# A decoder block with a 16,384-expert mixer: 16 tokens gathered on eight partitions each in place of 32 on four

## The chip, the cores and the metric

The kernel runs on one core of one Trainium2 chip. The metric is the device time of one launch in microseconds (us). Engine names are those of the profile: PE is the matrix engine (PEld its weight loads), DVE the vector engine, ACT the scalar engine, POOL the general engine GpSimd, SP the engine that only issues transfers. Engines run their own instruction queues in order and meet at semaphores.

## The reference, cut to what matters

512 tokens of width 2048 go through a mixing block (gated projections and windowed attention) and then through a PEER layer: each token has 8 heads of 16 chosen experts out of 16,384, and each expert is one row of `expert_down` and one of `expert_up` (2048 values each).

```
q = (h @ w_query).reshape(T, 8, 2, 128)             # scores against 2 x 128 sub keys
...                                                 # top 16 of each half, top 16 of their sums
experts = e1 * 128 + e2;  gates = softmax(top_v)
u  = expert_down[experts]                           # (token, 8, 16, 2048)
a  = gelu(einsum('cd,chkd->chk', h, u))
vt = expert_up[experts]
out = einsum('chk,chkd->cd', gates * a, vt)
```

All is float32. A residual sum and a last normalization follow.

## The kernel before

Tokens are treated in one of two ways.

**Dense.** For `TD` = 352 tokens (`TD = TL - EX`, three blocks of 128 less the last `EX` = 32 tokens) the kernel multiplies with all experts. The 16,384 experts are 128 blocks of 128. `down(b)` multiplies block b of `expert_down` with the `TD` token columns and takes the gelu. `up(c)` multiplies eight blocks (a chunk) of `expert_up` with the gelus, each first multiplied by a gate table g that is zero where a token did not choose the expert. In `up` there are four quarters q; each has four weight pieces, and adds its result into `accT`. Every float32 product is three matmuls of split operands (`mm3`, lines 166 to 168: high by high, high by low, low by high). So each `down` and each eighth of a chunk is 48 matmuls with a moving operand of 128 partitions by `TD` columns.

**Gathered.** The first block of 128 tokens, and the `EX` tokens left over, are done row by row instead. One *unit* is one half row (1024 values) on 128 partitions: GpSimd issues an indirect transfer (line 706, 512 KB), and DVE either multiplies and sums it against the token (`expert_down`, line 720) or adds it, weighted, into `half_row` (`expert_up`, line 732). For the first block a partition is a token, with 128 experts, so 4 x 128 = 512 units. For the `EX` = 32 tokens, each is spread over P // EX = 4 partitions with 32 experts each: 4 x 32 = 128 units, and `finish_last` adds the four partial sums at the end.

**The weight stream** (class `Stream`). Weights come in pieces of 128 x 1024 (512 KB) through SP into `wraw` (4 buffers). ACT casts a piece to its high part `whi` (line 143), and DVE or GpSimd subtracts to get the low part `wlo` (line 145); four buffers each. `W.get(ahead)` hands out a piece and first issues the splits of up to `ahead` more pieces (2 by default). 24 matmuls use one piece.

**The pacer** (class `Pace`). The order of the work beside the matmuls is laid out when the program is built. Each `mm3` credits `vector` with 0.98 of its planned matmul time (3 x columns x 0.4505 ns), and everything on DVE is charged in planned ns. While `vector` is positive the pacer issues the table work (`paced`, when due), one unit per `gap`, or other leftovers. A split goes to DVE when `vector` is positive (charge 1250), else to GpSimd (charge 500). From the last gate table on, `spread` sets `gap` so that the units left are spread evenly over the matmuls left.

**The stages.** First the mixing block, the projections and the choice of experts. Then `down` of blocks 0 to 87 (`NPRE` = 88); beside the first 83 of them (`OPEN`) the gate tables are made for the dense tokens, four tokens at a time (a quad: four DVE products at line 860, eight small matmuls at line 873) and stored in `g_dram`, `NTG` groups of 32 tokens. The gelus of these 88 blocks go out to `a_dram`. Then chunks 0 to 9 of `up`, one after the other, for which gelus and tables are loaded back and multiplied (`make_ga`: the product at line 994, the cast at 998, the low part at 999). From block 88 on eight `down` and one `up` alternate, and `make_ga` is called in `down`. In the last chunk, `finish_first` (its second part is `rest_of_first`) finishes the first block, `finish_last` the `EX` tokens, and `rows_out` turns `accT` back into rows, adds and normalizes.

## Time and profile before

| | us |
|---|---|
| median of 3 runs (lowest, highest) | 3057.38 (3054.41, 3064.22) |
| the profiled execution | 3053.1 |
| its span, first to last instruction | 3051.4 |
| PE busy | 2867.4 (94%) |
| DVE busy | 2260.2 (74%) |
| POOL busy | 1474.2 (48%) |
| ACT busy | 1152.7 (38%) |
| mean granted clock of PE | 0.976 |

The profiled execution is 4.3 us below the median. Busy times are unions of an engine's instructions; those of PE are partly modelled, since matmuls overlap in the pipeline, so the pace of the matmuls is better read from the distance between their starts. A group's row gives its busy time, the mean duration of one, and the idle time just before its instructions with what ended it.

### The profile page before, as it was taken

How to read it: one execution, taken by the hardware profiler on the slowest of the kernel's cores; microseconds unless marked ns; L12 is line 12 of the kernel's file. 1: busy time of each engine (PE TensorE's matmuls, PEld its weight loads, DVE VectorE, ACT ScalarE, POOL GpSimd, SP SyncE). 2: the span in 40 equal slices, each digit the busy share in tenths (PEclk: the TensorE clock that was granted, in tenths of full speed). 3: DMA queues.
4: the chain of work that ended last, by engine and by line, in shares of the span. 5: the costliest groups of instructions: out<-in, count | busy, mean ns of one | idle time of the engine just before them, and what ended most of it. 6: DMA issues, size and time to landing. Idle time of an engine off the chain costs nothing. (4 is left out here: it accounts for less than half of the span.)

```text
span 3051.4 us, 44502 instructions
## 1 busy us (share of the span) xinstructions
PE 2867.4 (94%) x16925; PEld 2727.1 (89%) x16925; DVE 2260.2 (74%) x3359; ACT 1152.7 (38%) x1932; POOL 1474.2 (48%) x998
## 2 busy tenths in 40 slices
PE   7999999999999899999989999999999999999976
PEld 6888878799999899999988999998999999999975
DVE  3125642469947999999957888887788889778865
ACT  3244432222333456767824222322232323323223
POOL 2132100123578667777645666666665444344432
PEclk9999999999999999999999999999999999999987
DMA  5221242422379678978798999999989999899983
GB/s 191 86 83 56 76 162 90 146 90 87 122 260 343 215 264 293 317 261 316 264 333 323 357 347 342 337 334 329 353 330 347 334 334 360 315 332 335 347 306 104
DMA packets 265190, 779.91 MB, mean 256 GB/s; under 512 B 25488, under 2 KB 94416, under 8 KB 259408
## 3 DMA queue, kind: packets, MB, share of 16 engines
q1 hardware_dynamic: 151952, 382.75, 36.7%
q0 software_dynamic: 92160, 335.59, 29.0%
q10 hardware_dynamic: 20864, 58.74, 5.0%
q8 instruction: 133, 2.18, 0.3%
q14 instruction: 81, 0.66, 0.1%
HBM read 726.20 MB, written 50.77 MB: 255 GB/s over the span
## 5 line engine op out<-in xcount | busy, mean ns | idle before, releaser
L145 POOL TENSOR_TENSOR wlo<-wraw,whi 128x1024 fp32r<-128x1024 f32 x284 | 701.0, 2477 | 849.1 <-ACT whi L143 813.3
L143 ACT CAST whi<-wraw 128x1024 fp32r<-128x1024 f32 x628 | 641.2, 1048 | 679.3 <-PE up L167 326.8
L168 PE MATMUL up<-gah,wlo 128*128 128x352 f32 x2048 | 673.9, 329 | 47.2 <-POOL wlo L145 44.0
L166 PE MATMUL up<-gah,whi 128*128 128x352 f32 x2048 | 675.2, 330 | 19.9 <-DVE accT L1092 19.2
L145 DVE TENSOR_TENSOR wlo<-wraw,whi 128x1024 fp32r<-128x1024 f32 x344 | 462.1, 1350 | 305.5 <-ACT whi L143 303.8
L166 PE MATMUL dn<-h2d,whi 128*128 128x352 f32 x2048 | 667.3, 326 | 15.2 <-ACT whi L143 15.2
L168 PE MATMUL dn<-h2d,wlo 128*128 128x352 f32 x2048 | 669.7, 327 | 5.8 <-POOL wlo L145 3.6
L167 PE MATMUL up<-gal,whi 128*128 128x352 f32 x2048 | 668.9, 327 | 0.0
L167 PE MATMUL dn<-h2d,whi 128*128 128x352 f32 x2048 | 667.0, 326 | 0.0
L168 PEld LDWEIGHTS up<-gah,wlo 128*128 128x128 f32 x2048 | 394.0, 192 | 56.9 <-POOL wlo L145 53.2
L166 PEld LDWEIGHTS up<-gah,whi 128*128 128x128 f32 x2048 | 394.4, 193 | 27.5 <-DVE accT L1092 18.0
L166 PEld LDWEIGHTS dn<-h2d,whi 128*128 128x128 f32 x2048 | 390.8, 191 | 16.1 <-ACT whi L143 16.1
L168 PEld LDWEIGHTS dn<-h2d,wlo 128*128 128x128 f32 x2048 | 389.5, 190 | 10.3 <-POOL wlo L145 6.9
L167 PEld LDWEIGHTS up<-gal,whi 128*128 128x128 f32 x2048 | 394.7, 193 | 0.0
L167 PEld LDWEIGHTS dn<-h2d,whi 128*128 128x128 f32 x2048 | 389.7, 190 | 0.0
L720 DVE SCALAR_TENSOR_TENSOR row<-row,half_row 128x1024 f32<-128x1024 f32 x236 | 282.6, 1211 | 70.0 <-DMA row<-in_down_rows,idx 55.7
L860 DVE SCALAR_TENSOR_TENSOR p<-iota,eT,gT 128x256 fp32r<-128x256 f32 x352 | 317.0, 959 | 1.9 <-PE tr L873 1.9
L706 POOL DMA_INDIRECT row<-in_down_rows,idx x236 | 249.3, 1056 | 140.5 <-DVE row L720 88.7
L706 POOL DMA_INDIRECT more<-in_up_rows,idx x160 | 184.4, 1152 | 162.0 <-DVE half_row L732 136.3
L706 POOL DMA_INDIRECT row<-in_up_rows,idx x160 | 182.9, 1143 | 145.3 <-DVE half_row L732 115.7
L732 DVE SCALAR_TENSOR_TENSOR half_row<-more,wgt,half_row 128x1024 f32<-128x1024 f32 x160 | 205.1, 1282 | 1.5 <-DMA more<-in_up_rows,idx 0.3
L732 DVE SCALAR_TENSOR_TENSOR half_row<-row,wgt,half_row 128x1024 f32<-128x1024 f32 x156 | 200.0, 1282 | 1.7 <-DMA row<-in_up_rows,idx 0.3
(201 smaller groups left out, 3755.7 us busy)
## 6 DMA issues: line engine op xcount, KB each, us to landing
wraw<-in_down SPq DMA_DIRECT2D x256, 512.0 KB, 5.6
wraw<-in_up SPq DMA_DIRECT2D x256, 512.0 KB, 7.0
wraw<-in_win SPq DMA_DIRECT2D x52, 512.0 KB, 3.8
g_dram<-stage ACTq DMA_DIRECT2D x22, 1024.0 KB, 8.2
g<-g_dram SPq DMA_DIRECT2D x32, 704.0 KB, 9.3
wraw<-in_wout SPq DMA_DIRECT2D x32, 512.0 KB, 3.7
wraw<-in_wq SPq DMA_DIRECT2D x32, 512.0 KB, 3.7
aa<-a_dram SPq DMA_DIRECT2D x88, 176.0 KB, 9.1
```

Of the source, the lines that this page charges most:

```text
L143: self.nc.scalar.copy(hi, src)
L145: eng.tensor_sub(lo, src, hi.bitcast(F32))
L166: nc.tensor.matmul(ps, wh, xh, start=start, stop=False)
L167: nc.tensor.matmul(ps, wh, xl, start=False, stop=False)
L168: nc.tensor.matmul(ps, wl, xh, start=False, stop=stop)
L706: nc.gpsimd.indirect_dma_start(out=t, out_offset=None, in_=src, in_offset=bass.IndirectOffsetOnAxis(ap=idx[i][:, j, h:h + 1], axis=0))
L720: nc.vector.scalar_tensor_tensor(t, t, 1.0, half_row, op0=OP.mult, op1=OP.mult, accum_out=dots[i][:, j, h:h + 1])
L732: nc.vector.scalar_tensor_tensor(half_row, t, wgt[i][:, j:j + 1], half_row, op0=OP.mult, op1=OP.add)
L860: nc.vector.scalar_tensor_tensor(p2[:, j], iota[:, None, :].to_broadcast([P, 2, P]), t[:, 1, k:k + 1], hl[:, k, :, None].to_broadcast([P, ...
```

## The change

`EX` becomes 16 and `TD` so 368. The 16 tokens are spread over eight partitions each with 16 experts each, which makes 4 x 16 = 64 units in place of 128 (576 in all in place of 640). 368 is eleven and a half groups of 32, so there are 12 groups in `g_dram`; the last is half filled, its rest set to zero by GpSimd, and `make_ga` multiplies the last 16 columns on GpSimd and the other 352 on DVE. `NPRE` goes to 80 and `OPEN` to 75: chunks 0 to 8 run in a row, and from block 80 on `down` and `up` alternate. Buffers for gathered rows in the later stages go from 4 + 4 to 4 + 3. The pacer's first gap is 2800 ns, a split goes to DVE already when `vector` is over -400, and in each quarter of `up` the pacer issues nothing beside the last two column groups (`held`). `down` and the first half of each quarter of `up` ask for splits three pieces ahead. In the last chunk `rest_of_first` moves from the second quarter to the third; `finish_last` loads the partial sums as two transfers of 128 partitions and adds the eight parts with a matmul against a matrix of ones in place of eight DVE additions.

```diff
-EX = 32
+EX = 16
 TD = TL - EX
-NPRE = 88
+NPRE = 80
 OPEN = NPRE - 5
-NTG = TD // TG
+NTG = -(-TD // TG)
+FULL = TD // TG
-MORE_ROWS = 4
+MORE_ROWS = 3
...
-        self.gap = 2600.0
+        self.gap = 2800.0
...
-        if self.vector > 0.0 or self.pool < 0.0:
+        if self.vector > -400.0 or self.pool < 0.0:
             self.vector -= 1250.0
...
+                            used = TD - b * P - 4 * n
+                            if used < TG:
+                                nc.gpsimd.memset(stage[h][:, :, used:], 0.0)
...
-                    if n % 8 == 7:
+                    if n % 8 == 7 or 4 * (n + 1) == TD - b * P:
...
-        t3 = t.rearrange("p (g t) -> p g t", g=NTG)
         g = g4[b // 4][:, :, (b % 4) * TG:(b % 4 + 1) * TG]
-        nc.vector.tensor_tensor(t3, t3, g, op=OP.mult)
+        if FULL < NTG:
+            end = t[:, FULL * TG:]
+            nc.gpsimd.tensor_tensor(end, end, g[:, FULL, :TD - FULL * TG], op=OP.mult)
+        t3 = t[:, :FULL * TG].rearrange("p (g t) -> p g t", g=FULL)
+        nc.vector.tensor_tensor(t3, t3, g[:, :FULL], op=OP.mult)
...
-            hi, lo = W.get()
+            hi, lo = W.get(3)
...
-                w = W.get()
+                w = W.get(3)
...
-            if last and q == 1:
+            if last and q == 2:
                 rest_of_first()
-            if last and q == 2:
                 pace.drain()
                 rest_of_last = finish_last()
...
             for m in range(4):
+                pace.held = m > 1
...
+            pace.held = False
...
-            for s in range(P // EX):
-                ...
-                eng.dma_start(t[:n], y_dram[1][s * n:(s + 1) * n, cols])
-                parts.append((t, cols))
+            t = pg.tile([P, D // 2], F32, name="row", bufs=4)
+            nc.sync.dma_start(t, y_dram[1][:, h * D // 2:(h + 1) * D // 2])
+            parts.append(t)
+        ones = late["fin"].tile([P, EX], F32, name="ones")
+        nc.vector.tensor_reduce(ones, ident.rearrange("p (s m) -> p m s", m=EX), axis=AX.X, op=OP.add)
...
-            for t, cols in parts:
-                nc.vector.tensor_add(x[:n, cols], x[:n, cols], t[:n])
             for q in range(4):
+                cols = slice(q * 512, (q + 1) * 512)
+                ps = ps2.tile([P, 512], F32, name="dn", bufs=2)
+                nc.tensor.matmul(ps[:n], ones, parts[q // 2][:, q % 2 * 512:(q % 2 + 1) * 512],
+                                 start=True, stop=True)
+                nc.vector.tensor_add(x[:n, cols], ps[:n], x[:n, cols])
```

## Rows read from the trace of the kernel before

**Rows 1.** The page: span, busy time of three engines, and the span in 40 slices (granted clock of PE, busy share of the transfer engines, in tenths).

```profile
span 3051.4 us, 44502 instructions
...
PE 2867.4 (94%) x16925; PEld 2727.1 (89%) x16925; DVE 2260.2 (74%) x3359; ACT 1152.7 (38%) x1932; POOL 1474.2 (48%) x998
...
PEclk9999999999999999999999999999999999999987
DMA  5221242422379678978798999999989999899983
```

**Rows 2.** Busy time by engine in stretches of the span, the boundaries being the first matmuls of a stage: stretch, length, busy us of each engine (and instructions), granted clock, busy share of the transfer engines, GB/s.

```profile
0.00:784.00 784.00, 751.46 (x3877) 637.83 (x3877) 378.40 (x908) 264.50 (x460) 151.93 (x96) 1.00 0.30 106
784.00:1541.00 757.00, 734.11 (x4702) 728.82 (x4702) 674.87 (x992) 430.50 (x886) 559.05 (x318) 0.98 0.78 271
1541.00:1593.40 52.40, 41.59 (x239) 39.76 (x237) 29.83 (x45) 13.04 (x19) 17.63 (x16) 0.90 0.99 372
1593.40:2287.60 694.20, 643.96 (x3840) 630.85 (x3841) 564.79 (x717) 208.74 (x261) 429.94 (x301) 0.97 0.91 339
2287.60:2929.10 641.50, 622.43 (x3842) 618.20 (x3841) 542.71 (x619) 200.00 (x245) 288.41 (x242) 0.99 0.93 337
2929.10:3029.80 100.70, 72.40 (x425) 70.72 (x423) 63.19 (x71) 30.33 (x53) 25.03 (x22) 0.85 0.51 184
3029.80:3051.40 21.60, 1.41 (x9) 0.92 (x9) 6.41 (x12) 5.61 (x9) 2.21 (x6) 0.58 0.37 134
```

**Rows 3.** Matmul groups over the span (line, tiles, shapes, count; busy us, mean ns of one, overlapping; idle before), and in the timeline the first and last of ten matmuls in a row with 384 columns (start, duration).

```profile
L166 PE MATMUL up<-gah,whi 128*128 128x352 f32 x2048 | 675.2, 330 | 19.9 <-DVE accT L1092 19.2 <-ACT whi L143 0.4 <-ACT accT L1090 0.3
L166 PE MATMUL dn<-h2d,whi 128*128 128x352 f32 x2048 | 667.3, 326 | 15.2 <-ACT whi L143 15.2
L1145 PE MATMUL dn<-ident,accT 128*128 128x128 f32 x32 | 4.4, 274 | 0.3 <-DVE accT L1092 0.3
...
700.16 0.34 PE L166 MATMUL acc<-h2d,whi 128*128 128x384 f32 x1
...
701.72 0.34 PE L166 MATMUL acc<-h2d,whi 128*128 128x384 f32 x1
```

**Rows 4.** The timeline of ACT: the gelus that end a `down`, first and last of eight in a row in the late stage, and two neighbours beside the tables.

```profile
2371.72 0.47 ACT L1037 ACTIVATE aa<-dn 128x352 f32<-128x352 f32 x1 [6.79 <-PE dn L168]
...
2425.48 0.46 ACT L1037 ACTIVATE aa<-dn 128x352 f32<-128x352 f32 x1 [2.26 <-PE dn L168]
1443.29 0.47 ACT L1033 ACTIVATE asp<-dn 128x352 f32<-128x352 f32 x1 [0.45 <-PE dn L168]
1452.77 0.46 ACT L1033 ACTIVATE asp<-dn 128x352 f32<-128x352 f32 x1 [0.45 <-PE dn L168]
```

**Rows 5.** Who waited for whom in the stretch of the ten chunks, 1593 to 2287 us: total, times, longest.

```profile
DVE gal L999 <- ACT gah L998: 49.7, 81, 2.5
PE up L168 <- POOL wlo L145: 39.4, 22, 3.8
PE up L166 <- DVE accT L1092: 10.1, 11, 2.6
```

**Rows 6.** Groups of DVE and of POOL in the same stretch.

```profile
L145 DVE TENSOR_TENSOR wlo<-wraw,whi 128x1024 fp32r<-128x1024 f32 x89 | 147.2, 1659 | 37.1 <-ACT whi L143 36.7
L732 DVE SCALAR_TENSOR_TENSOR half_row<-row,wgt,half_row 128x1024 f32<-128x1024 f32 x69 | 88.4, 1282 | 0.9 <-DMA row<-in_up_rows,idx 0.3
L1092 DVE TENSOR_TENSOR accT<-up,accT 128x352 f32<-128x352 f32 x142 | 72.7, 518 | 39.1 <-PE up L168 38.8
L994 DVE TENSOR_TENSOR aa<-aa,g 128x352 f32<-128x352 f32 x81 | 46.6, 575 | 0.0
L999 DVE TENSOR_TENSOR gal<-aa,gah 128x352 fp32r<-128x352 f32 x81 | 42.5, 525 | 49.7 <-ACT gah L998 49.7
L145 POOL TENSOR_TENSOR wlo<-wraw,whi 128x1024 fp32r<-128x1024 f32 x72 | 173.0, 2414 | 167.2 <-ACT whi L143 139.9 <-issue 18.1 <-PE up L167 8.5
```

**Rows 7.** Groups of DVE and POOL in the alternating stage, 2287 to 2929 us.

```profile
L145 DVE TENSOR_TENSOR wlo<-wraw,whi 128x1024 fp32r<-128x1024 f32 x156 | 189.9, 1220 | 38.1 <-ACT whi L143 37.3 <-PE dn L168 0.9
L706 POOL DMA_INDIRECT more<-in_up_rows,idx x84 | 98.8, 1176 | 121.8 <-DVE half_row L732 113.9 <-DVE more L720 4.2 <-DVE wlo L145 2.2
```

**Rows 8.** Groups of DVE and of POOL beside the first `down` blocks, 784 to 1593 us.

```profile
L860 DVE SCALAR_TENSOR_TENSOR p<-iota,eT,gT 128x256 fp32r<-128x256 f32 x352 | 317.0, 959 | 1.9 <-PE tr L873 1.9
L720 DVE SCALAR_TENSOR_TENSOR row<-row,half_row 128x1024 f32<-128x1024 f32 x160 | 191.9, 1211 | 54.7 <-DMA row<-in_down_rows,idx 54.5
L145 POOL TENSOR_TENSOR wlo<-wraw,whi 128x1024 fp32r<-128x1024 f32 x162 | 403.7, 2497 | 158.0 <-ACT whi L143 156.5
```

**Rows 9.** The last chunk: the timeline of DVE where `rest_of_first` and `finish_last` run, and what PE waited for from 2929 us on.

```profile
2963.82 2.29 DVE L1160 TENSOR_TENSOR yf<-yf,xf 128x2048 f32<-128x2048 f32 x1 [7.72 <-DMA xf<-x_dram]
...
2972.84 0.75 DVE L1128 TENSOR_SCALAR yf<-yf,rstd 128x1024 f32<-128x1024 f32 x1 [3.51 <-POOL rstd L1126]
...
3004.48 4.95 DVE L1184 TENSOR_TENSOR xf<-xf,more 32x1024 f32<-32x1024 f32 x4
3009.36 4.95 DVE L1184 TENSOR_TENSOR xf<-xf,row 32x1024 f32<-32x1024 f32 x4
...
PE dn L1145 <- DVE xr L1148: 25.6, 4, 16.1
```

**Rows 10.** The small transfers that spread the last tokens' indices, on SP: duration least, median, most (ns), first and last start.

```profile
L931 SPq DMA_DIRECT2D idx<-e_dram x4: 302/416/422, 1374.8 to 1378.0; - x4
```

More of the change, by code (lines that the diff above doesn't have):

```diff
@@ L1171, in finish_last @@
         for h in range(2):
-            cols = slice(h * D // 2, (h + 1) * D // 2)
-            for s in range(P // EX):
-                if h:
-                    t = pg.tile([P, D // 2], F32, name="row", bufs=4)
-                else:
-                    t = late["p"].tile([P, D // 2], F32, name="more", bufs=MORE_ROWS)
-                eng = nc.sync if s % 2 else nc.scalar
-                eng.dma_start(t[:n], y_dram[1][s * n:(s + 1) * n, cols])
-                parts.append((t, cols))
+            t = pg.tile([P, D // 2], F32, name="row", bufs=4)
[3 more added lines that the diff above has]
+        nc.vector.tensor_reduce(ones, ident.rearrange("p (s m) -> p m s", m=EX), axis=AX.X, op=OP.add)
         def rest():
-            for t, cols in parts:
-                nc.vector.tensor_add(x[:n, cols], x[:n, cols], t[:n])
             for q in range(4):
+                cols = slice(q * 512, (q + 1) * 512)
[3 more added lines that the diff above has]
+                nc.vector.tensor_add(x[:n, cols], ps[:n], x[:n, cols])
                 square(NB, n, x, q, nc.vector)
```

## Prediction

> **What bounds the kernel now.** I read the page first. PE is busy 94% of the span at a clock of nearly 2.4 GHz throughout [rows 1]; so PE is the engine to account for, but its busy time is modelled, and I asked the starts of matmuls instead.
>
> In the late stage eight gelus that end a `down` lie 53.76 us apart from first to last [rows 4]: 7.68 us for 48 matmuls, 160.0 ns for one of 352 columns. That is a pace without any gap. Ten matmuls of 384 columns lie 1.56 us apart from first to last, 173.3 ns each [rows 3]. So 32 columns cost 13.3 ns (one column per cycle of 2.4 GHz), on top of a fixed 13.3 ns, and 160 ns is no floor under which 352 columns happen to lie.
>
> With that I split the span [rows 2] into what PE needs without gaps and what is lost.
>
> - 0 to 784 us, before the experts: 784.0, hardly touched.
> - 784 to 1593.4, 88 `down` and the tables: 809.4. The `down` need 88 x 7.68 = 675.8. Beside the tables two neighbours end 9.48 us apart [rows 4], 1.80 more than 7.68 for two quads, so 0.90 per quad and 78.8 for 88 quads (I take 0.895). Lost: 54.8.
> - 1593.4 to 2287.6, ten chunks: 694.2, needed 10 x 61.44 = 614.4. Lost: 79.8, or 8.0 a chunk.
> - 2287.6 to 2929.1, 40 `down` and five chunks: 641.5, needed 614.4. Lost: 27.1.
> - 2929.1 to 3029.8, the last chunk and the rows out: 100.7, needed 61.4. Lost: 39.3.
> - 21.6 of tail.
>
> About 200 us are thus lost after 784 us. Where are they? In the ten chunks PE waits 39.4 us in 22 waits for low parts that GpSimd splits, and 10.1 for DVE's additions into `accT` [rows 5]; the granted clock there is 0.97 [rows 2], so another 3% of 694, 21 us, go to half clock after such waits. In the alternating stage, with nearly every split on DVE, 156 of them [rows 7], little is lost. In the last chunk 25.6 us are waits of the row transposes for DVE [rows 9], which sits 7.7 us on a late transfer and then does 9.9 us of additions.
>
> **The change, part by part.** *Columns.* 352 to 368 adds 16 / 2.4 = 6.67 ns: 166.7 a matmul, 8.00 us a `down`, 64.0 a chunk. For 2 x 6144 matmuls (2048 of each of the three kinds, twice [rows 3]) that is 81.9 us, wherever PE has no gap to put it in. This is the cost that everything else has to earn back.
>
> *Tables.* 92 quads in place of 88: 3.6 us on PE. On DVE 16 more products of 0.96 us [rows 8], 15 us, in a stage where DVE is busy 675 of 757 us [rows 2].
>
> *Eight `down` later.* 80 `down` before the chunks take 640.0, and the quads 82.3. DVE has less time there: the pacer's plan for the table stage goes from 83 x 7.61 = 632 to 75 x 7.96 = 597 us. Quads come first, so units give way. About 150 units are done before the spread now (160 in the first four buffers up to the chunks [rows 8]). Plan time falls 34, the quads take 8 more, splits on GpSimd 8 less, and the new threshold sends perhaps a quarter of 150 splits to DVE, at 0.75 more each some 20 to 28: together 54 to 62 us, or 43 to 49 units of 1.26. I take 107 units done. The losses of the stage should stay: 52 of 54.8, since one piece more of splits at hand shortens the waits a little. The 16 small index transfers of the last tokens in place of eight cost SP 8 x 0.42 = 3.4 us [rows 10], which four loaded pieces cover. Sum: 774.3.
>
> *Units.* 576 - 107 = 469 are left at the spread, before about 490. The gap is (8304 x 352 x 0.4505 ns - 45 us) / 490 = 2.60 us now and (8688 x 368 x 0.4505 ns - 45 us) / 469 = 2.98 us after. That is where the 16 tokens fewer arrive: 21.4 units a chunk in place of 23.
>
> *Splits.* In a chunk of the row of ten, the plan credits 59.7 us now and charges 8 x 1.06 for `make_ga`, 16 x 0.52 for `accT`, 23 x 1.26 units and 16 x 1.25 splits: 65.8. The 6.1 too many divided by 0.75 is eight splits sent to GpSimd; the trace has 72 in ten chunks [rows 6], so the arithmetic holds. After: credit 62.4, charges 63.8, so two. GpSimd takes 2.41 us for a split [rows 6] behind its gathers, so most of the 39.4 us should go. I keep a third: 1.3 a chunk, 0.8 of half clock, 0.5 for `accT` (the held pacer helps), and 0.4 for DVE.
>
> *DVE in a chunk.* That last term is the bound from the other side. A split on DVE takes 1.66 us in the stage where GpSimd splits too [rows 6] and 1.22 where it hardly does [rows 7]. The stage after is nearer to the second; with 1.25 the 14 splits are 17.5, units 21.4 x 1.28 = 27.4, `make_ga` 8 x 1.10 = 8.8, `accT` 16 x 0.52 = 8.3, and the wait of line 999 for the cast 49.7 / 10 = 5.0 [rows 5, 6]: 67.0. So DVE needs 67.0 and PE 64.0 + 3.0. I take 67.0 a chunk, 603.0 for nine; with 1.66 a split it would be 72.7. The Trainium skill ("SBUF — State Buffer", section "Who interferes with whom") says that a DVE instruction with two SBUF inputs contends with a GpSimd instruction that reads SBUF, one blocking the other for its whole length; rows 6 and 7 agree, and by that rule the 0.44 us shrink with the splits on GpSimd, from seven to two, to some 0.12, so 1.34 a split and 68 a chunk.
>
> *The strip on GpSimd.* No row shows a product of 128 x 16 there. In line it costs nothing if GpSimd is early, as it is: in the late stage it waits 121.8 us for DVE to free row buffers [rows 7]. At worst it stands behind a gather, 1.18 us [rows 7], or a split, 2.41 [rows 6], with the cast and line 999 behind it. I take nothing, and keep the worst as a rival. The 4 + 3 row buffers leave five units of 2.98 us ahead, enough; no cost.
>
> *Alternating stage.* 48 `down` and six chunks: 768.0. Half rows come more seldom and splits are asked for earlier, against twice as many small transfers at the change to the last tokens' units: 18 lost of 27 before, 786.0.
>
> *Last chunk.* `rest_of_first` one quarter later finds its data: the 7.7 us go, the 7.5 from the end of its addition to that of its scaling [rows 9] stay. Eight additions of 9.9 become four of about 0.7: 7.0 go. Half clock after these waits: 2 go. The matmul against ones is 4 x 512 columns of full float32; by the transposes, 4.4 / 32 = 0.14 us for 128 columns [rows 3], four times 0.55, 2.2 in all (between 0.9, at the pace of split operands, and that). 64.0 + 39.3 - 16.7 + 2.2 = 88.8.
>
> **The sum.** 784.0 + 774.3 + 603.0 + 786.0 + 88.8 + 21.6 = 3057.7, against 3051.4: +6.3. The profiled execution took 1.7 more than its span, 3053.1; on the median, 3057.4, it is 3063.7. I predict 3064 us: the price of the columns is almost earned back.
>
> **Rivals.** *The losses nearly vanish (faster).* If DVE keeps ahead of PE without GpSimd, as in the alternating stage, a chunk takes 65.0: 585. With a third of the losses before the chunks gone too the first stage takes 760, the alternating stage 778, the last chunk 82. That is 3011 of span, 3017 on the median. For it: 22 waits make most of the loss of ten chunks, and GpSimd ends them. Against it: DVE's 67.0. It decides once DVE's chunk is under 65, five units fewer or the cast's wait hidden. One reason more: held units and earlier splits are in better order, which I can't price from rows.
>
> *GpSimd keeps splitting.* If fewer units are done beside the tables than I think, the gap is short again. With 70 done it is 2.76 us, 23.1 units a chunk, five splits on GpSimd, and DVE at 1.5 us a split; a chunk is 71 to 72 and the table stage 785: 3115 on the median.
>
> *The strip stalls (slower).* With 1.18 us of wait in each `make_ga`, nine chunks take 8 x 1.18 x 9 = 85 us more, since DVE has no slack there, less what overlaps: 3110 to 3150. From 0.1 us a product on, 7 us, it makes the kernel measurably slower.
>
> *Transfers as the bound.* A chunk moves 69.4 us x 339 GB/s = 23.5 MB now; with two units less and slightly larger tables 22.8, in 67 us 340 GB/s, which the stage has now, and the stage after the tables ran at 372 [rows 2]. No rival of its own.
>
> **Chances and range.** Forecast (3040 to 3085) 0.40; losses vanish (3000 to 3040) 0.34; GpSimd keeps splitting (3085 to 3125) 0.16; the strip stalls (over 3090) 0.10. Within 0.3% of the median, about what a measurement of this kernel can tell, lie 3048 to 3067. Of the forecast's 0.40, 0.06 lie under it, 0.20 in it, 0.14 above. So faster 0.40, same 0.20, slower 0.40. The range from 3002 to 3112 leaves out some 0.05 below and 0.12 above.
>
> **What would show it.** A `down` without tables every 8.00 us; were it 7.7, the columns would be free. GpSimd's splits in the chunks: about two each, and the wait of PE for them under 15 us. Chunks of 67 us with DVE over 90% busy. In `make_ga`, the cast waiting for DVE and not for POOL. In the last chunk, no wait for `xf` and a stall of PE under 10 us at the third quarter. Wrong it will be, most likely, in the losses: I keep 52 + 27 + 18 + 23 of 200 us, and each is an estimate.

## The result, and the profile after

The changed kernel takes 3094.59 us (median; 3092.09 to 3097.35) beside 3057.38 for the kernel before on the same chip (3054.41 to 3077.88): 1.011 times as long, 95% interval 1.0087 to 1.0132. The forecast was 3064, in a range from 3002 to 3112. The profiled execution took 3092.45, with a span of 3090.7: 39.3 more than before and 33.0 more than the sum.

The head of the page after, beside [rows 1]: PE is busy longer by 82 us, DVE and GpSimd are busy less by 121 and 221, and the program is nevertheless longer.

```profile
span 3090.7 us, 44663 instructions
...
PE 2949.0 (95%) x16965; PEld 2815.8 (91%) x16965; DVE 2139.4 (69%) x3362; ACT 1175.2 (38%) x1960; POOL 1253.6 (41%) x978
```

The same stretches as [rows 2], in its columns: before the experts; 80 `down` and the tables (two rows); nine chunks; alternating stage; last chunk; tail.

```profile
0.00:785.10 785.10, 751.17 (x3876) 637.42 (x3877) 357.06 (x827) 264.58 (x460) 144.38 (x93) 1.00 0.30 105
785.10:1488.00 702.90, 691.86 (x4305) 689.98 (x4304) 573.07 (x1030) 417.88 (x872) 405.66 (x224) 0.99 0.70 245
1488.00:1539.90 51.90, 48.59 (x286) 47.45 (x285) 25.85 (x39) 18.45 (x35) 20.77 (x22) 0.97 0.99 363
1539.90:2159.70 619.80, 593.03 (x3458) 583.62 (x3457) 475.82 (x704) 190.38 (x238) 326.23 (x290) 0.99 0.88 325
2159.70:2956.00 796.30, 783.33 (x4609) 781.63 (x4609) 631.47 (x676) 247.45 (x295) 315.24 (x307) 0.99 0.87 308
2956.00:3072.50 116.50, 79.58 (x433) 74.74 (x431) 69.61 (x78) 30.84 (x53) 39.09 (x36) 0.82 0.57 217
3072.50:3090.70 18.20, 1.41 (x9) 0.93 (x9) 6.52 (x13) 5.62 (x9) 2.23 (x6) 0.58 0.45 166
```

To read them I need the pace without gaps first. In the timeline of PE (start, duration) the first and last of the 384 matmuls of one chunk in the alternating stage, with no gap between them, are

```profile
2304.96 0.33 PE L167 MATMUL up<-gah,whi 128*128 128x368 f32 x1
...
2369.43 0.33 PE L169 MATMUL up<-gah,wlo 128*128 128x368 f32 x1
```

64.47 us for 383 steps, 168.3 ns each, so a chunk of 384 needs 64.63 us and not 64.0. Two gelus on ACT, five `down` apart, beside [rows 4]:

```profile
2256.52 0.48 ACT L1044 ACTIVATE aa<-dn 128x368 f32<-128x368 f32 x1 [3.17 <-PE dn L169]
...
2297.05 0.48 ACT L1044 ACTIVATE aa<-dn 128x368 f32<-128x368 f32 x1 [3.17 <-PE dn L169]
```

40.53 / 5 = 8.106 us a `down`, 168.9 ns a matmul. With 8.107 and 64.63 (before 7.68 and 61.44), and 0.895 for each quad, PE's work without gaps is known; what is left of the length of each stretch is loss:

| us | before: length, lost | forecast: length, lost | after: length, lost |
|---|---|---|---|
| before the experts | 784.0 | 784.0 | 785.1 |
| `down` and tables | 809.4, 54.8 | 774.3, 52 | 754.8, 23.9 |
| chunks in a row | 694.2, 79.8 | 603.0, 27 | 619.8, 38.2 |
| alternating | 641.5, 27.1 | 786.0, 18 | 796.3, 19.4 |
| last chunk and tail | 122.3, 60.9 | 110.4, 46.4 | 134.7, 70.1 |

The losses fell by 71 us, from 222.6 to 151.6. The columns took more than that: 12,288 matmuls by some 8.6 ns (8.9 in `down`, 8.3 in `up`) are 106 us, the four quads 3.6. 109 - 71 + 1 is the 39 us. So the kernel is slower not because something new went wrong in the middle, but because PE has 109 us more to do and only 71 us of its gaps were closed.

The 61.44 of a chunk before is the prediction's: it took `down`'s 160.0 ns for `up` too. Chunks without a gap at 352 columns are a little faster, as in the run "Both undone" below (first and last of 384):

```profile
2384.20 0.33 PE L167 MATMUL up<-gah,whi 128*128 128x352 f32 x1
...
2445.22 0.32 PE L169 MATMUL up<-gah,wlo 128*128 128x352 f32 x1
```

61.02 / 383 = 159.3 ns, 61.2 us a chunk. So the columns cost some 110 us and not 106, and the losses before were some 4 us larger than the table says, which leaves the sum as it is. I keep 61.44, to compare with the prediction.

The next readings say where gaps closed and where not. Waits in the nine chunks, beside [rows 5]: PE's wait for low parts from GpSimd went from 39.4 us in 22 to 14.2 in seven, and a new one stands in `make_ga`, the cast (`gah`) waiting for the strip's product on GpSimd (line 999). Most of the cast's waiting is still for DVE's product (line 1001).

```profile
ACT gah L1005 <- DVE aa L1001: 144.7, 54, 8.2
ACT gah L1005 <- POOL aa L999: 37.8, 10, 4.2
PE up L169 <- POOL wlo L146: 14.2, 7, 2.0
PE up L167 <- DVE accT L1099: 6.4, 9, 0.9
```

Groups of DVE and POOL in the same stretch, beside [rows 6]: 37 splits are on GpSimd, four a chunk, and the strip's product takes 390 ns.

```profile
L146 DVE TENSOR_TENSOR wlo<-wraw,whi 128x1024 fp32r<-128x1024 f32 x108 | 134.0, 1256 | 15.7 <-ACT whi L144 15.6
L146 POOL TENSOR_TENSOR wlo<-wraw,whi 128x1024 fp32r<-128x1024 f32 x37 | 95.6, 2594 | 169.5 <-ACT whi L144 169.4
L999 POOL TENSOR_TENSOR aa<-aa,g 128x16 f32<-128x16 f32 x73 | 26.9, 390 | 12.8 <-DMA wraw<-in_up 7.4 <-DMA aa<-a_dram 4.9
```

Groups of the table stage, 785 to 1540, beside [rows 8]: DVE's table product fell from 959 to 670 ns, with 115 splits on GpSimd in place of 162.

```profile
L861 DVE SCALAR_TENSOR_TENSOR p<-iota,eT,gT 128x256 fp32r<-128x256 f32 x368 | 222.8, 670 | 6.6 <-PE tr L874 6.6
L146 DVE TENSOR_TENSOR wlo<-wraw,whi 128x1024 fp32r<-128x1024 f32 x44 | 56.6, 1287 | 80.8 <-ACT whi L144 80.8
L146 POOL TENSOR_TENSOR wlo<-wraw,whi 128x1024 fp32r<-128x1024 f32 x115 | 288.1, 2507 | 258.8 <-ACT whi L144 258.2
```

And the last chunk, the timeline of DVE at the third quarter, beside [rows 9]: `rest_of_first` finds `xf` at once (line 1168 has no wait), but then ten units (line 733) come one behind the other, 3014.8 to 3030.3, three of them waiting for their rows. Only after them does the row's residual (`xr`) run.

```profile
3005.07 2.28 DVE L1168 TENSOR_TENSOR yf<-yf,xf 128x2048 f32<-128x2048 f32 x1
...
3014.15 0.75 DVE L1136 TENSOR_SCALAR yf<-yf,rstd 128x1024 f32<-128x1024 f32 x1 [3.52 <-POOL rstd L1134]
3014.82 1.28 DVE L733 SCALAR_TENSOR_TENSOR half_row<-more,wgt,half_row 128x1024 f32<-128x1024 f32 x1
3016.14 5.26 DVE L733 SCALAR_TENSOR_TENSOR half_row<-row,wgt,half_row 128x1024 f32<-128x1024 f32 x4
3021.64 1.29 DVE L733 SCALAR_TENSOR_TENSOR half_row<-more,wgt,half_row 128x1024 f32<-128x1024 f32 x1 [0.23 <-DMA more<-in_up_rows,idx]
3023.98 2.68 DVE L733 SCALAR_TENSOR_TENSOR half_row<-more,wgt,half_row 128x1024 f32<-128x1024 f32 x2 [1.05 <-DMA more<-in_up_rows,idx]
3027.65 2.66 DVE L733 SCALAR_TENSOR_TENSOR half_row<-row,wgt,half_row 128x1024 f32<-128x1024 f32 x2 [0.99 <-DMA row<-in_up_rows,idx]
3030.49 1.28 DVE L1156 TENSOR_TENSOR xr<-dn,xr 128x512 f32<-128x512 f32 x2
```

What PE waited for from 2956 us on says what that cost: 33.5 us, 26.1 of it in one piece at this place; before, 25.6 and 16.1 [rows 9].

```profile
PE dn L1153 <- DVE xr L1156: 33.5, 4, 26.1
```

### The profile page after: what moved, and what is told of

Read it like the earlier page. It is cut to its first block, busy times and chain, and to the rows that moved or that the text cites. A ratio compares the mean times of both kernels' runs of the same rounds, so it can differ in the third digit from the quotient of the medians.

```text
span 3090.7 us, 44663 instructions
## 1 busy us (share of the span) xinstructions
PE 2949.0 (95%) x16965; PEld 2815.8 (91%) x16965; DVE 2139.4 (69%) x3362; ACT 1175.2 (38%) x1960; POOL 1253.6 (41%) x978
## 4 chain that ended last, share of the span: by engine, by line
PE 38%; DVE 4%; issue 3%; DMA 2%; POOL 2%; ACT 1%; SPq 0%; ACTq 0%; POOLq 0%; DVEq 0%
PE up L169 9%; PE up L167 8%; PE up L168 8%; PE dn L167 4%; PE dn L169 4%; PE dn L168 4%; DMA wraw<-in_up 1%; DVE wlo L146 1%; POOL wlo L146 1%; DVE row L721 1%; DVE half_row L733 1%; DVE accT L1099 0%; DMA more<-in_up_rows,idx 0%; POOL row L707 0%; DMA row<-in_up_rows,idx 0%
## 5 line engine op out<-in xcount | busy, mean ns | idle before, releaser
L146 POOL TENSOR_TENSOR wlo<-wraw,whi 128x1024 fp32r<-128x1024 f32 x198 | 498.9, 2526 | 972.8 <-ACT whi L144 970.5
L146 DVE TENSOR_TENSOR wlo<-wraw,whi 128x1024 fp32r<-128x1024 f32 x430 | 533.0, 1251 | 376.3 <-ACT whi L144 376.0
L167 PE MATMUL up<-gah,whi 128*128 128x368 f32 x2048 | 685.2, 335 | 20.9 <-ACT whi L144 13.6
L169 PE MATMUL up<-gah,wlo 128*128 128x368 f32 x2048 | 684.6, 334 | 18.9 <-POOL wlo L146 17.5
L167 PE MATMUL dn<-h2d,whi 128*128 128x368 f32 x2048 | 685.4, 335 | 4.2 <-ACT whi L144 2.5
L169 PE MATMUL dn<-h2d,wlo 128*128 128x368 f32 x2048 | 680.6, 332 | 5.2 <-POOL wlo L146 4.5
L168 PE MATMUL up<-gal,whi 128*128 128x368 f32 x2048 | 682.2, 333 | 0.0
L168 PE MATMUL dn<-h2d,whi 128*128 128x368 f32 x2048 | 677.8, 331 | 0.0
L1099 DVE TENSOR_TENSOR accT<-up,accT 128x368 f32<-128x368 f32 x240 | 126.7, 538 | 150.5 <-PE up L169 150.5
L861 DVE SCALAR_TENSOR_TENSOR p<-iota,eT,gT 128x256 fp32r<-128x256 f32 x368 | 222.8, 670 | 6.6 <-PE tr L874 6.6
L707 POOL DMA_INDIRECT more<-in_up_rows,idx x125 | 141.0, 1128 | 126.4 <-DVE half_row L733 105.6
```

The costliest lines, as they stand in the source:

```text
L146: eng.tensor_sub(lo, src, hi.bitcast(F32))
L167: nc.tensor.matmul(ps, wh, xh, start=start, stop=False)
L168: nc.tensor.matmul(ps, wh, xl, start=False, stop=False)
L169: nc.tensor.matmul(ps, wl, xh, start=False, stop=stop)
L707: nc.gpsimd.indirect_dma_start(out=t, out_offset=None, in_=src, in_offset=bass.IndirectOffsetOnAxis(ap=idx[i][:, j, h:h + 1], axis=0))
L861: nc.vector.scalar_tensor_tensor(p2[:, j], iota[:, None, :].to_broadcast([P, 2, P]), t[:, 1, k:k + 1], hl[:, k, :, None].to_broadcast([P, ...
```

## The experiments

Theory at the start: the columns are paid in full and the units saved don't earn them back; the rest of the change is a gain. Rivals: the strip's wait; units left for the end; the lower threshold for splits; too small a gap for three pieces ahead. Edits are against the changed kernel, ratios against the kernel before, and "lost" is counted as in the table above. The kernels ran on several chips, each beside the kernel before, so the ratios compare them; their intervals are 0.002 to 0.006 wide on either side, and stretches are read from one execution of each kernel.

**Fewer tokens undone.** Everything else of the change stays.

```diff
-EX = 16
+EX = 32
```

> The changed kernel with EX back at 32 (352 dense columns, 128 units for the last tokens) and every other part of the change kept. Theory (the columns are the cost: 168.9 ns for 368 columns against 160.0 for 352, 8.9 ns times 12288 matmuls = 109 us, while the 64 units saved were mostly hidden): a down goes back to 7.68 us and a chunk to a floor of 61.4; the stage beside the tables 717 us, nine chunks some 607, the alternating stage 757, the last chunk and tail 134, in all about 3000 us, faster than both kernels. Rival (the units bound the stages, so taking 64 of them away was a gain and the scheduling parts are the loss): the time stays at 3080 us or more.

Measured 3078.63 us, 1.0053 (1.0032 to 1.0074): 16 faster than the changed kernel, not 95. The theory missed, and the rival nearly came true. 47 units fall into the last stage (23 in the changed kernel); it takes 165.7 us, and PE waits 58.8 in it for `xr`. (The window of the last stage with the tail, then PE's wait in it.)

```profile
2906.40:3072.10 165.70, 79.80 (x442) 73.37 (x440) 107.45 (x116) 36.46 (x63) 63.10 (x64) 0.75 0.64 249
```
```profile
PE dn L1153 <- DVE xr L1156: 58.8, 4, 53.7
```

Something else in the change thus costs a kernel with 32 tokens a great deal. Two places could be it, the end and the splits.

**Units spread to end sooner.** The margin in `spread` doubled.

```diff
-        pace.gap = (left * TD * COL_NS - 45e3) / len(pace.units)
+        pace.gap = (left * TD * COL_NS - 90e3) / len(pace.units)
```

> The changed kernel with the spread's margin at 90 us in place of 45, so that units come every 2.88 us of plan and not 2.98 and end earlier. Theory (ten units left over are run in a row in the third quarter of the last chunk, and PE stands still for 26.4 us there): no units left there, the stall falls by some 13 us to about 13, the time to about 3081 us. Rival (the units only move: in the chunks they push splits to GpSimd): the last chunk gains 13 us and the nine chunks lose as much, 3090 to 3096 us.

Measured 3082.04, 1.006 (1.0037 to 1.0083). 16 units in the last stage, last stage and tail 124.2 in place of 134.7, PE's wait for `xr` 21.5 in place of 33.5; the nine chunks 623.7, 3.9 more. That is near the 3081 of the theory, but the stall stays at 14.6. So units that are late are a cost of the end, but moving them gives back part of it elsewhere.

**The old threshold for splits**, alone.

```diff
-        if self.vector > -400.0 or self.pool < 0.0:
+        if self.vector > 0.0 or self.pool < 0.0:
```

> The changed kernel with splits going to DVE only when the pacer's vector credit is over 0, as before. Theory (GpSimd's splits slow the two-input operations of DVE beside the tables: the product at line 861 took 0.67 us after and 0.96 before): the product goes back to about 0.9 us, GpSimd splits 150 pieces beside the tables, that stage takes 770 to 780 us in place of 755, and the chunks have seven splits on GpSimd and not five; the time is 3110 to 3130 us. Rival (the stage is shorter only because eight blocks left it): it stays within 3 us of 755, and the time within 0.3% of the changed kernel's.

Measured 3078.62, 1.0054 (1.0014 to 1.0093), 16 less than the changed kernel where I expected more. (Windows of tables and of the last stage; DVE's table product and GpSimd's splits beside the tables.)

```profile
785.10:1542.40 757.30, 741.57 (x4589) 738.49 (x4588) 643.18 (x989) 438.60 (x907) 519.30 (x298) 0.99 0.76 266
2962.40:3076.90 114.50, 80.17 (x442) 74.53 (x440) 62.24 (x80) 35.48 (x61) 31.50 (x32) 0.85 0.51 196
```
```profile
L861 DVE SCALAR_TENSOR_TENSOR p<-iota,eT,gT 128x256 fp32r<-128x256 f32 x368 | 289.7, 848 | 12.6 <-PE tr L874 12.5
L146 POOL TENSOR_TENSOR wlo<-wraw,whi 128x1024 fp32r<-128x1024 f32 x148 | 368.3, 2492 | 178.1 <-ACT whi L144 176.8 <-issue 0.2
```

DVE is slower at the tables again, yet that stage ends only 2.5 us later; the chunks take 7.8 more, the alternating stage 3.9 less, and the last stage 20.2 less, with 14 units in it. So the faster products of DVE, which the theory took for the gain beside the tables, are worth 2.5 us there; the rival, within 3 us of 755, holds for that stage. DVE's time, which the lower threshold spends on splits, is time that units then lack: 123 units are done before the spread with the old threshold, 107 with the new one.

**Both undone.**

```diff
-EX = 16
+EX = 32
...
-        if self.vector > -400.0 or self.pool < 0.0:
+        if self.vector > 0.0 or self.pool < 0.0:
```

> The changed kernel with EX back at 32 and with the old threshold (splits go to DVE only with credit over 0); every other part of the change kept. With EX = 32 alone 48 units were left for the last chunk, which took 165.6 us with its tail, and the table stage 726, nine chunks 617, the alternating stage 778. Theory (the threshold charges DVE for splits and so pushes units to the end, and units in the last chunk run while PE stands still): few units are left, the last chunk and its tail take 120 to 125 us, the chunks about 69 each as before the change (621), the table stage about 735, in all 3030 to 3045, faster than both kernels. Rival (the units left come from the 128 units themselves, whatever the threshold): the last chunk stays over 150 us and the time over 3060.

Measured 3031.08, 0.9898 (0.9840 to 0.9957): faster than both kernels. The time lies where the theory put it, but not for its reason: 35 units are left, the last stage takes 149.3 and not 120 to 125, and it is the nine chunks that are short, 598.9 and not 621. (The windows of tables, nine chunks, alternating stage, last and tail.)

```profile
783.90:1526.70 742.80, 714.42 (x4557) 705.75 (x4556) 631.07 (x948) 426.05 (x878) 495.54 (x278) 0.98 0.74 259
1526.70:2125.60 598.90, 574.40 (x3457) 565.97 (x3456) 476.47 (x677) 188.47 (x237) 378.23 (x260) 0.97 0.93 341
2125.60:2879.90 754.30, 739.87 (x4611) 738.00 (x4610) 638.12 (x718) 244.51 (x296) 389.32 (x317) 0.99 0.95 349
2879.90:3029.20 149.30, 81.12 (x441) 74.67 (x439) 88.70 (x101) 36.23 (x62) 56.71 (x55) 0.76 0.60 233
```

So the rest of the change (80 blocks beside the tables, three pieces ahead, the buffers and the new end) is worth 22.2 us of span against the kernel before (1.0%, some 31 us, by the medians on its chip). The 39.3 us of the change divide into -22.2 for that, +47.7 for the 16 tokens made dense, columns and units together, at the old threshold (3029.2 to 3076.9), and +13.8 for the threshold on top. In the other order the threshold costs 42.9 at 32 tokens and the 16 tokens 18.6 on top: the two don't add up to a fixed price each.

Losses at the old threshold show what 64 units fewer, beside wider matmuls, do to the gaps. In the order tables, chunks, alternating, end:

| us | gapless | lost | sum of losses |
|---|---|---|---|
| 32 tokens, old threshold | 7.68, 61.44 | 49.6, 45.9, 17.0, 87.9 | 200.4 |
| 16 tokens, old threshold | 8.107, 64.63 | 26.4, 46.0, 15.5, 49.9 | 137.8 |

62.6 us fewer lost, 109 paid for: that is the price of the tokens. 38.0 of the gain come in the last stage, where 35 units fall with 32 tokens and 14 with 16; in the nine chunks fewer units gain nothing. The 23.2 beside the tables can't come from fewer units, since more are done there: 135 of line 721 with 16 tokens, 123 with 32. PE's work without gaps grows by 37.7 us in that stage and its length by 14.5, and PE waits less for DVE's products (32 tokens, then 16):

```profile
PE tr L874 <- DVE p L861: 8.1, 15, 2.6
PE tr L874 <- DVE p L861: 3.8, 6, 2.5
```

So wider matmuls seem to give the other engines time that they lacked there. No run changes the columns without the units, so this is argued and not shown.

**What a column costs.** A small kernel without the block: nothing but runs of split matmuls, eight widths.

```diff
+SIZES = (320, 336, 344, 352, 360, 368, 376, 384)
...
+    for n in (512, *SIZES):
+        ...
+            for k in range(16):
+                ...
+                mv = [x[i][:, k % 4, :m] for i in range(2)]
+                nc.tensor.matmul(ps[:, :m], w[0][:, s], mv[0], start=k == 0, stop=False)
+                ...
```

> A small kernel that leaves the whole block out and only runs groups of 96 matmuls, three per weight pair as in the kernel, with 320, 336, 344, 352, 360, 368, 376 and 384 columns. Theory A (straight line between 352 and 384): starts lie 160.0, 163.3, 166.7, 170.0 and 173.3 ns apart from 352 to 384. Theory B (column counts that are no multiple of 32 pay extra): 368 takes 168.9 ns as in the changed kernel, 2.2 over the line, and 360 and 376 lie over it too. Theory C (what slows 368 in the changed kernel is other engines' traffic): 368 takes 166.7 here.

The moving rows `x` lie 1536 bytes apart. Measured, from the first and last start of 96 in a row (94 for 320): 146.6 ns for 320, 153.4 for 336, 157.8 for 344, 161.1 for 352, 164.5 for 360, 166.7 for 368, 173.3 for 376, 173.4 for 384. (Timeline of PE, 368 and 376 columns.)

```profile
105.82 0.33 PE L38 MATMUL ps<-x,w 128*128 128x368 f32 x1
...
121.66 0.33 PE L40 MATMUL ps<-x,w 128*128 128x368 f32 x1
121.82 0.33 PE L38 MATMUL ps<-x,w 128*128 128x376 f32 x1
...
138.28 0.33 PE L40 MATMUL ps<-x,w 128*128 128x376 f32 x1
```

15.84 / 95 and 16.46 / 95. The prediction's 166.7 is right for this layout, and not what the changed kernel shows. The steps from 352 on are 3.4, 2.2, 6.6 and 0.1 ns for eight columns each, so there is no straight line: theory A fails at 376, B at 368, and C is left for the next runs.

**Where the rows lie.** The same, with rows 1536 bytes apart from byte 0 or from byte 32 (`from_flat(8)`), rows of 368 packed one behind the other, and cases with copies on ACT and subtractions on DVE meant to run beside (`traffic`).

```diff
+    cases = [..., (368, from_flat(0), None), ..., (352, from_flat(8), None),
+             (368, from_flat(8), None), ..., (368, from_pack, None),
+             ..., (368, from_flat(0), traffic), ..., (368, from_flat(8), traffic), ...]
```

> A small kernel that leaves the whole block out, as the one with eight column counts; there 368 columns took 166.7 ns and in the changed kernel 168.9. Here 96 matmuls each with 368 and with 352 columns whose moving rows begin 0 or 32 bytes past a multiple of 64 in the buffer (the changed kernel's h2d rows begin 32 past one), with rows packed 368 apart (as the changed kernel's gah), and with ACT and DVE copying other tiles beside them. Theory (the place of the rows): 368 takes 168.9 ns with the 32 byte offset or with packed rows and 166.7 without, copying or not, and 352 takes 160 to 161 in each. Rival (the other engines' traffic): 168.9 only beside the copies. If neither shows it, the 2.2 ns stay unexplained.

Measured for 368: 166.7 from byte 0, 167.8 from byte 32, 168.8 packed; in the cases with `traffic` 166.6 from byte 0 and 166.7 from byte 32. For 352: 161.1 from byte 0, 160.0 from byte 32 both times. For 384 173.4 always. (Timeline of PE, first and last of 96: from byte 0, then packed. Timeline of DVE and of ACT: all subtractions of `traffic`, and its last copies.)

```profile
63.58 0.33 PE L60 MATMUL ps<-flat,w 128*128 128x368 f32 x1
...
79.42 0.33 PE L62 MATMUL ps<-flat,w 128*128 128x368 f32 x1
144.33 0.33 PE L60 MATMUL ps<-pack,w 128*128 128x368 f32 x1
...
160.37 0.33 PE L62 MATMUL ps<-pack,w 128*128 128x368 f32 x1
...
7.21 37.70 DVE L46 TENSOR_TENSOR busy<-busy,busy 128x1024 f32<-128x1024 f32 x30
...
41.03 6.46 ACT L45 COPY busy<-busy 128x1024 f32<-128x1024 f32 x6
```

The traffic ended at 47.5 us, before any matmul with 368 columns began (63.6). So it ran only beside the first ones with 384 columns, which from 18 us on took the same 173.4, and the cases that bear its name are repeats without it. What this run shows is the packed rows: 2.1 ns over rows 1536 bytes apart from byte 0, as the theory had it; the rival was not tested at this width. From byte 32 two runs of 368 differ by 1.1 ns, so that place is not settled. `gah` and `gal` are packed, 1472 bytes apart. `h2d` is not: its rows are 1536 bytes apart, beginning 32 bytes past a multiple of 64, for which this kernel shows 166.7 and 167.8 and `down` 168.9. That difference stays open, and for `down` other engines' traffic is not ruled out.

**Rows of `gah` and `gal` padded** to 384 columns in the changed kernel.

```diff
-        hi = late["p"].tile([P, TD], F32R, name="gah", bufs=10)
-        lo = late["p"].tile([P, TD], F32R, name="gal", bufs=10)
+        hi = late["p"].tile([P, TL], F32R, name="gah", bufs=10)[:, :TD]
+        lo = late["p"].tile([P, TL], F32R, name="gal", bufs=10)[:, :TD]
```

> The changed kernel with the gah and gal rows 384 apart in the buffer in place of 368, nothing else. Theory (packed rows of 368 cost 168.8 ns a matmul in the small kernel, rows 384 apart 166.8): the chunks of the alternating stage go from 64.6 to 64.0 us, the sixteen chunks together gain some 10 to 13 us, the time is about 3080 us; the down stay at 8.1. Rival (2 ns are lost elsewhere when one matmul gets shorter, since other engines set the pace): the time within 0.2% of the changed kernel's.

Measured 3086.07, 1.0067 (1.0047 to 1.0088), 8.5 less. (Timeline of PE, first and last of the 384 of a chunk, 383 steps.)

```profile
2302.71 0.33 PE L167 MATMUL up<-gah,whi 128*128 128x368 f32 x1
...
2366.55 0.33 PE L169 MATMUL up<-gah,wlo 128*128 128x368 f32 x1
```

63.84 / 383 = 166.7 ns, while `down` keeps its 168.9. That is the pace of the small kernel with nothing beside, so for `up` it was the place of the rows and not the traffic of the other engines. 6144 x 1.65 ns is 10.1 us, and most of it arrives.

**The strip back on DVE.**

```diff
-            nc.gpsimd.tensor_tensor(end, end, g[:, FULL, :TD - FULL * TG], op=OP.mult)
+            nc.vector.tensor_tensor(end, end, g[:, FULL, :TD - FULL * TG], op=OP.mult)
```

> The changed kernel with the product of the last 16 columns in make_ga on DVE in place of GpSimd. In the changed kernel ACT's cast waits 37.8 us in the chunks and 32.9 in the alternating stage for GpSimd's strip. Theory (ACT is idle there and the cast is early enough, so the wait is hidden): the time stays within 0.3% of the changed kernel's, DVE having 128 short products more. Rival (the strip is what keeps a chunk at 68.9 us over a floor of 64.9): chunks of 66 to 67 us, 15 to 25 us faster.

Measured 3082.05, 1.0066 (1.0042 to 1.0090): 12.5 less than the changed kernel, between the theory (within 9) and the rival (15 to 25). The nine chunks take 611.5 in place of 619.8, the alternating stage 792.4 in place of 796.3, and PE's wait for GpSimd's low parts is 7.5 in place of 14.2. The 37.8 us that the cast waits for the strip are thus mostly covered; about one microsecond a chunk is not.

**Two pieces ahead in place of three.**

```diff
-            hi, lo = W.get(3)
+            hi, lo = W.get(2)
...
-                w = W.get(3)
+                w = W.get(2)
```

> The changed kernel with splits asked for two pieces ahead, as before. Theory (asked for earlier, a split stands ahead of units, gathers and make_ga in its engine's queue): PE's waits for split parts in the chunks and the alternating stage rise from about 31 us to 45 or more, the time to 3105 to 3115. Rival (four buffers limit the splits in either case, since a split can't begin before PE has left the piece four back): no difference beyond 0.3%.

Measured 3112.40, 1.0170 (1.0109 to 1.0230), as the theory expected. The whole difference stands in the nine chunks, 638.0 in place of 619.8, where PE waits 22.2 us for DVE's splits (0.9 in the changed kernel) and 12.5 for GpSimd's.

```profile
PE up L169 <- DVE wlo L146: 22.2, 11, 3.3
PE up L169 <- POOL wlo L146: 12.5, 16, 1.7
```

So with two pieces ahead DVE's splits come late, and with three in time. That they then stand behind units is my reading of the order on DVE; I didn't count it.

**Nothing held back** in the quarters of `up`.

```diff
-                pace.held = m > 1
+                pace.held = False
```

> The changed kernel without the hold (the pacer issues beside the last two column groups of a quarter as well). Theory (the hold keeps units from standing before the additions into accT, and costs nothing): PE's waits for accT in the chunks rise from 6.4 to 15 us or more and the time by 5 to 15 us. Rival (the hold is what leaves ten units for the last chunk): the last chunk falls from 134.7 us with its tail to about 120, and the time falls by 5 to 15 us.

Measured 3078.25, 1.0043 (1.0021 to 1.0066). Both halves of what was expected are there: nine chunks 641.4 (+21.6), with PE waiting 17.1 for additions into `accT` in place of 6.4; alternating stage 787.0 (-9.3); last and tail 113.5 (-21.2), with seven units. The stage beside the tables is 5.5 shorter as well. Holding pays in a row of chunks and costs where the units have to be finished; in the sum it costs this kernel 14.5 us of span.

**Fast kernel with a wider margin** (the two edits of "Both undone", and a margin of 120 in place of 45 us).

```diff
-        pace.gap = (left * TD * COL_NS - 45e3) / len(pace.units)
+        pace.gap = (left * TD * COL_NS - 120e3) / len(pace.units)
```

> The changed kernel with EX at 32, the old threshold, and a margin of 120 us in place of 45 in the spread. With the first two alone the time was 3031, and 35 units ran from the last chunk on, which took 149 us with its tail; PE waited 40 us there for DVE. Theory (the units left over are what the last chunk pays for): hardly any are left, the last chunk and tail take 122 to 128 us, the rest up to 8 us more, in all 3005 to 3018. Rival (units come no earlier, or cost as much in the chunks as they save at the end): 3025 to 3035.

Measured 3046.91, 0.9941 (0.9916 to 0.9967), 16 more than without; theory and rival both missed. The end falls from 149.3 to 129.9 (17 units), but the chunks rise from 598.9 to 615.2 and the alternating stage from 754.3 to 769.8: a unit squeezed into the chunks costs no less than one left over.

**Fast kernel, held only in the row of chunks** (the two edits of "Both undone", and this one).

```diff
-                pace.held = m > 1
+                pace.held = m > 1 and nxt is not None
```

> The kernel of the run with EX at 32 and the old threshold (3031 us), with the hold kept in the nine chunks that run in a row and dropped in the later ones. Without any hold the changed kernel's nine chunks rose from 619.8 to 641.3 us, while its alternating stage fell from 796.4 to 787.0 and its last chunk from 115.6 to 94.4. Theory (the hold earns its keep only where make_ga stands on DVE beside the additions, and elsewhere it delays units into the last chunk): nine chunks stay at 599 (595 to 605), the alternating stage falls from 754 to 745 to 752, the last chunk from 127 to 100 to 110, in all 3000 to 3015. Rival (in the alternating stage the hold is needed at 128 units for the last tokens as well): PE's waits for accT there rise from 1.2 us to over 10 and the time stays within 0.3% of 3031.

Measured 3033.35, 0.9916 (0.9890 to 0.9941): no gain; the alternating stage takes 759.2 in place of 754.3, and the end is 149.3 again, with 33 units. The theory that holding in the alternating stage makes the units late falls for 32 tokens, and the rival's sign isn't there either, since PE waits 3.6 us for `accT` in that stage and not over 10. What makes the units late stays open.

## Why the prediction was right and wrong

Its line of thought, the columns against the gaps, is what happened, and the time lies in its range. The sum is 33.0 us short, and these are its terms:

| us | sum | measured | of the 33.0 |
|---|---|---|---|
| 368 columns without gaps | 8.00, 64.0 | 8.107, 64.6 | +23.7 |
| losses beside the tables | 52 | 23.9 | -28.1 |
| losses of nine chunks | 27 | 38.2 | +11.2 |
| losses, alternating | 18 | 19.4 | +1.4 |
| last chunk and tail, beyond a chunk's matmuls | 46.4 | 70.1 | +23.7 |
| before the experts | 784.0 | 785.1 | +1.1 |

That the whole is no further off is partly luck: the gain beside the tables, which the sum did not have, hides 28.1 of the 61.1 us that the other terms are short.

**Columns: a wrong size.** "16 / 2.4 = 6.67 ns" took the step from 352 to 384 [rows 3, 4] as a straight line. The width sweep gives 166.7 for 368 where rows are 1536 bytes apart from byte 0, but there 352 has 161.1 and the steps between are uneven, so that the line meets it by luck; packed rows cost 168.8, and `down` has 168.9. Padding brought `up` back to 166.7, which shows the cause for that half; `down`'s stays open. With 160.0 against 168.6 the columns cost 106 us (110 with `up`'s own 159.3), not 81.9. They arrive in full in the chunks (at the old threshold 28.7 us more work without gaps, 28.7 more time) and nearly so in the alternating stage (39.6 and 38.1), but not beside the tables (37.7 and 14.5).

**Tables: losses not kept.** The step "the losses of the stage should stay" failed. At the old threshold they fell from 49.6 to 26.4 us when 16 tokens became dense, though PE's work grew; that wider matmuls give the other engines time there, as said above, is argued and not shown. The threshold took another 2.5 (26.4 to 23.9); at 32 tokens it is worth 16.6 there (742.8 to 726.2). It acts through a thing that the prediction left out, what sending splits from GpSimd to DVE does to DVE's other work. DVE's table product takes 959 ns beside 162 splits on GpSimd, 904 and 848 beside 148 (32 tokens, 16 tokens, old threshold), 730 beside 121 (32 tokens, new threshold), 670 beside 115. From before to after 368 products are 106 us shorter, against 44 splits on DVE of 1.29, 57 us, where there were 12. The Trainium skill ("SBUF — State Buffer", section "Who interferes with whom") says that DVE instructions with two SBUF inputs contend with GpSimd instructions that read SBUF; the product has two, and these rows agree in direction (904 and 848 beside the same count show that the count isn't all). I had used the rule for splits in the chunks and not here. The count of units was exact: 107 of line 721 end before the spread. So the effect on the number of units was right, and those on PE's waits and on DVE's durations were left out.

**Nine chunks: DVE's work is not the bound.** The 67.0 came from DVE's work, "DVE over 90% busy". It is busy 475.8 of 619.8 us, 77%, so the sum of its work doesn't set a chunk's length; single waits of PE for it remain. GpSimd kept 37 splits where I expected some 18; the plan that gave two was an average, while the threshold is asked piece by piece, which I take for the reason and didn't test. A chunk loses 4.2 us; PE's waits for GpSimd's splits are 1.6 of it (14.2 / 9), and with the strip on DVE 0.9 of the loss goes, partly the same time. The wait of PE for GpSimd's low parts fell under 15 us, as written, but only just.

**Strip: the rival lived in part.** The cast waits mostly for DVE, 144.7 us in the nine chunks, but for POOL too, 37.8 us, where I wrote "and not for POOL". Of the 85 us of the rival some 8 reach PE in the chunks, by the run with the strip on DVE; the rest is covered.

**Last chunk: a term that was missing.** The gain at `xf` came; the eight additions went. But the third quarter begins with `pace.drain()`, which issues whatever units remain, and I had priced none. Of the 23 units in this stage ten were late, and PE's wait there is 26.1 us where I wrote "a stall under 10". Units in the last stage (groups of line 733 on DVE) beside PE's longest wait for `xr`, in nine of the kernels:

| units | 7 | 14 | 16 | 17 | 23 | 23 | 33 | 35 | 47 |
|---|---|---|---|---|---|---|---|---|---|
| longest wait, us | 7.9 | 10.7 | 14.6 | 10.7 | 26.1 | 26.4 | 34.7 | 36.7 | 53.7 |

From 14 units to 47 that is 43.0 / 33 = 1.30 us for each, the 1.29 of a unit on DVE, as a mean: between neighbours it goes from 0.9 to 1.7, and 17 units wait less than 16. So beyond some 14 a late unit lengthens PE's wait by about its whole duration; the kernel gains less by moving it (margin of 90), or loses (margin of 120). With 14, last chunk and tail take 114.5, near the 110.4 of the sum.

**Right:** 80 `down` before the chunks with 107 units; no `down` at 7.7 us; losses of the alternating stage; `rest_of_first` without a wait for `xf`. No run tests the small index transfers and the buffers, which I took as free. Of "held units and earlier splits", which I could not price, the splits are in better order: two pieces ahead cost 18 us more in the chunks. The hold is so in the chunks alone, where it saves 21.6; without it the whole is 14.5 us shorter.

The 0.40 for slower stood mostly on the wrong cases: neither splits kept on GpSimd nor the strip alone put the time where it is, but the columns' size and the late units. The time lies in the interval that I gave to GpSimd's splits (3085 to 3125), mostly by another cause: the four splits a chunk are near that rival's five, but 107 units were done beside the tables and not 70, and that stage took 754.8 and not 785.

## What to carry to other kernels

Work added to an engine was paid in full in the stages where it had few gaps, and in part where it waited for others; work taken from others came back only where a gap was waiting for it: write both down by stage before summing. A planner's threshold spends one engine's time, so ask who lacks it at the end of the list, and count what is late there. Price a new matmul width with the rows where they will lie.

## What the runs showed of the hardware

The pace of split float32 matmuls depends on where the moving rows lie: for 368 columns 166.7 ns with rows 1536 bytes apart from byte 0 and 168.8 packed, 1472 apart, and in the whole kernel 166.7 padded and 168.3 packed; for 352 161.1 from byte 0 and 160.0 from byte 32, each twice; 173.4 for 384 in both places. For 368 from byte 32 the two runs give 167.8 and 166.7. It is not straight in the columns: 376 cost the same as 384 (173.3, 173.4), and 368 6.6 less. Copies by ACT and subtractions by DVE beside 384 columns left them at 173.4; beside 368 the small kernels didn't test it. `down`'s 168.9 at rows of 1536 bytes, 32 bytes on, stays unexplained.
